# A decoder layer on one core: the last quarter of normed rows turned by transfers, and blocks, prepared sums and subtractions moved

## The chip, the core and the metric

The kernel runs on one core of one Trainium2 chip, as one program. The metric is the device time of one execution in microseconds, the median of several runs. The engines are named as in the profile: PE (TensorE, matmuls; PEld is its weight load), DVE (VectorE), ACT (ScalarE), POOL (GpSimd) and SP (SyncE, which here issues DMAs). A name such as L426 is a line of the kernel file.

## The reference

One layer of a decoder, all in float32, for 256 tokens (S) of width 2048 (D):

```
h = LN(alpha*h + 0.5*swiglu(h, w_ffn1_gu, w_ffn1_down))           # first feed-forward, FF = 5632
rq, rk, rv, rg, aq, ak, av, gate_r, gate_a = split(h @ w_in)
ro = head_norm(retention_chunkwise(rotary(rq), rotary(rk), rv))   # 8 heads, 128 / 256 wide
ret = (silu(rg) * ro) @ w_ret_out
att = sliding_window_attention_sinks(rotary(aq), rotary(ak), av) @ w_att_out
h = LN(alpha*h + (sigmoid(gate_r)*ret + sigmoid(gate_a)*att) @ w_mix_out)
h = LN(alpha*h + 0.5*swiglu(h, w_ffn2_gu, w_ffn2_down))
h = LN(alpha*h + sigmoid(h @ w_ple_gate) * (p @ w_ple_proj))
```

LN is a layer norm over the 2048 columns of a token, so a product that follows one needs the normed rows turned: tokens go from the partitions to the free axis.

## The kernel before, in words

**Products in three parts.** Each weight arrives by a DMA of 512 KB (128 partitions x 1024, "raw", `r...`), is cast on ACT to a rounded high part (`h...`, L130), and DVE subtracts to get the low part (`l...`, L134). A product is then three matmuls: high x high, high x low and low x high (L424 to L426), 512 columns each. A *pair* ("P") is two such chunks for one pair of k, 24 matmuls. A *transferred* unit ("T") has one of its two chunks get its low part in another way: ACT multiplies the raw weight by −1 (L139) and POOL issues a DMA that adds the raw weight (L140). A *seven* ("S") does the work of a pair with seven products in place of eight, 21 matmuls, from sums of weight quarters that DVE makes (`uf`, `vf`, `luf`, `lvf`, L214 to L223). A *prepared* unit ("D") is a seven whose sums were made earlier, in spare time, by `sums_ahead`, and put in DRAM.

**Stages.** First feed-forward: gate and up in eleven blocks of 512 columns (f1 j = 0 to 10, 5 to 459 us in the trace), down in two passes (to 689). Then the norm, the mixers (values `rv`, queries and keys `rqk`, gates `rg`, attention, `gt`, `ga`, `ma`, `mr`), the product with w_mix_out (`mo`, to 1446), a norm, the second feed-forward (f2, 1454 to 2136), a norm, and the embedding (`pg`, to the end). Each block of gate/up is given by a pattern of eight letters over the eight pairs of k (`gu_units`), for example PTSSPSST.

**Order.** Nothing is reordered at run time: each engine works through its instructions as written. A planner in the kernel's Python writes them. `plan` lists the units in the order in which PE uses them. After each unit that PE has been given, `fill` issues the next loads and the next casts and subtracts ("makes") as long as there is room (`slots_for_weights(slots, ahead, far)`: `ahead` is how many matmuls' worth of made weights may stand ready). Jobs put with `along(n, job)` and generators in `lazy` (tables, prepared sums) are given one step after each unit that PE has been given (`run_side`).

**A norm.** The class `Norm` combines the sums of a last block with the residual (`combine`), takes statistics, centres and scales the rows on DVE (`normal`, L660, L665), and turns them for the next product: PE transposes 128 x 128 pieces against an identity into PSUM (`lnps`, L677), ACT casts them to the high part (L105), DVE subtracts for the low part (L106). A norm has 16 such k for two halves of tokens, 32 transposes, in groups of four. These steps are put between the first matmuls of the next product by a list of events, (number of the step, what): a pair (t, c) is "turn quarter c of token half t", "more" centres and scales further rows, "go" lets `fill` run again. While a norm runs, that is held quiet. `held_out` runs the last block before a norm for one token half first, then for the other, so that the first half's norm can begin early.

**Turning by transfer.** Elsewhere (the blocks of the feed-forward, L947 to L967) rows are turned without PE: ACT copies the two 16-bit words of each value apart (`words_of`, L953), a transposing DMA on SP's queue turns them (`turn_words`, L959), and ACT joins the words (`join_words`, L967).

## Time and profile before

| | |
|---|---|
| median of 3 runs | 2243.78 us (2241.16 to 2244.8) |
| the profiled execution | 2240.34 us, span 2238.5 us, granted clock 0.999 |
| PE busy | 2226.3 us, 99% of the span, 10180 matmuls |
| DVE busy | 1992.1 us, 89%, 2646 instructions |
| ACT busy | 1414.8 us, 63%, 1672 instructions |
| POOL busy | 44.1 us, 2% |
| DMA | 558.71 MB, mean 250 GB/s; q1 (SP's loads) 71.0% and q0 (POOL's) 5.9% of 16 engines' span |

In rows of the timeline the columns are start, duration, engine, line, operation, out<-in, and in brackets how long the engine was idle ahead of it and what it waited for; several instructions of a kind in a row stand together (x8). In rows of waits they are the waiting engine, tile and line, who released it, and the time in total, the number of times and the longest. In rows of a tile they are durations in ns (least, median, largest), then first and last start. Names with a number (f19s, f210s) are feed-forward 1, block 9, and feed-forward 2, block 10; `s` is the PSUM bank of the sevens' products.

### The profile page before, as it was taken

The page shows a single profiled execution, that of the slowest core. Times are in us where ns is not written, and L with a number is a line of the kernel's source. Part 1 is how long each engine was busy: PE and PEld are TensorE (multiplying, and loading weights), DVE is VectorE, ACT ScalarE, POOL GpSimd, SP SyncE. Part 2 cuts the span into 40 slices and gives each one's busy share as a digit, 9 for nine tenths or more (in the row PEclk, how much of TensorE's full clock was granted, in tenths as well). Part 3 has the DMA queues.
Part 4 walks back from the last instruction along what each step waited for, and adds up shares of the span by engine and source line. Part 5 has one row for each costly group of instructions (what it writes and reads, how often), then busy time and mean ns, then how long its engine had stood idle before and what let it go on. Part 6 is the DMA issues. An engine that isn't in the chain of part 4 may idle for free.

```text
span 2238.5 us, 28874 instructions
## 1 busy us (share of the span) xinstructions
PE 2226.3 (99%) x10180; PEld 1842.2 (82%) x10180; DVE 1992.1 (89%) x2646; ACT 1414.8 (63%) x1672; POOL 44.1 (2%) x57
## 2 busy tenths in 40 slices
PE   9999999999999999999999999999999999999998
PEld 8888888888888888888788888788888888888887
DVE  7999999989999999898779778789998899899887
ACT  6776766786654644666866555456666677866543
POOL 0000000000000000000000000000000000000000
PEclk9999999999999999999999999999999999999999
DMA  9788887896776778986657569787979978867772
GB/s 315 227 261 244 226 259 234 229 262 235 253 273 260 252 266 308 305 257 205 189 165 248 172 215 326 263 291 253 314 250 273 311 233 248 262 224 252 284 268 72
DMA packets 288826, 558.71 MB, mean 250 GB/s; under 512 B 87964, under 2 KB 92444, under 8 KB 288680
## 3 DMA queue, kind: packets, MB, share of 16 engines
q1 hardware_dynamic: 279784, 529.11, 71.0%
q0 software_dynamic: 6912, 25.17, 5.9%
q10 hardware_dynamic: 1984, 2.58, 0.3%
q8 instruction: 80, 1.31, 0.2%
q14 instruction: 66, 0.54, 0.1%
HBM read 484.43 MB, written 29.36 MB: 230 GB/s over the span
## 4 chain that ended last, share of the span: by engine, by line
PE 88%; DVE 7%; DMA 3%; issue 2%; ACT 1%; ACTq 0%; DVEq 0%; POOL 0%; SPq 0%; POOLq 0%
PE rqk L375 3%; PE f1g L425 3%; PE f1g L424 3%; PE f1g L426 3%; PE f2g L425 2%; PE f2g L426 2%; PE f2g L424 2%; PE f1u L425 2%; PE f1u L424 2%; PE f1u L426 2%; PE f2u L425 2%; PE f2u L426 2%; PE f2u L424 2%; PE aqk L375 2%; PE gt L424 1%
## 5 line engine op out<-in xcount | busy, mean ns | idle before, releaser
L130 ACT CAST hf_gu<-rf_gu 128x1024 fp32r<-128x1024 f32 x264 | 271.3, 1046 | 44.4 <-DMA rf_gu<-in_f_gu 42.8
L134 DVE TENSOR_TENSOR lf_gu<-rf_gu,hf_gu 128x1024 fp32r<-128x1024 f32 x236 | 281.7, 1218 | 14.7 <-ACT hf_gu L130 13.4
L130 ACT CAST hf_down<-rf_down 128x1024 fp32r<-128x1024 f32 x145 | 148.4, 1047 | 61.4 <-DMA rf_down<-in_f_down 52.9
L134 DVE TENSOR_TENSOR lw_in_f<-rw_in_f,hw_in_f 128x1024 fp32r<-128x1024 f32 x140 | 167.1, 1218 | 3.5 <-ACT hw_in_f L130 3.3
L130 ACT CAST hw_in_f<-rw_in_f 128x1024 fp32r<-128x1024 f32 x140 | 141.9, 1050 | 24.9 <-DMA rw_in_f<-in_w_in_f 17.5
L134 DVE TENSOR_TENSOR lf_down<-rf_down,hf_down 128x1024 fp32r<-128x1024 f32 x125 | 149.6, 1218 | 7.6 <-ACT hf_down L130 6.9
L220 ACT CAST hvf_gu<-vf_gu 128x1024 fp32r<-128x1024 f32 x76 | 80.2, 1055 | 85.0 <-DVE vf_gu L219 77.2
L217 ACT CAST huf_gu<-uf_gu 128x1024 fp32r<-128x1024 f32 x76 | 80.0, 1053 | 54.5 <-DVE uf_gu L215 50.0
L222 DVE TENSOR_TENSOR luf_gu<-uf_gu,huf_gu 128x1024 fp32r<-128x1024 f32 x76 | 92.5, 1217 | 1.0 <-ACT huf_gu L217 1.0
L223 DVE TENSOR_TENSOR lvf_gu<-vf_gu,hvf_gu 128x1024 fp32r<-128x1024 f32 x76 | 92.5, 1217 | 0.0
L424 PE MATMUL f1g<-hf_gu,xt 128*128 128x512 f32 x232 | 90.7, 391 | 0.0
L426 PE MATMUL f1g<-lf_gu,xt 128*128 128x512 f32 x232 | 90.5, 390 | 0.0
L425 PE MATMUL f1g<-hf_gu,xt 128*128 128x512 f32 x232 | 90.5, 390 | 0.0
L424 PE MATMUL f2g<-hf_gu,ht 128*128 128x512 f32 x214 | 83.5, 390 | 0.0
L426 PE MATMUL f2g<-lf_gu,ht 128*128 128x512 f32 x214 | 83.3, 389 | 0.0
L425 PE MATMUL f2g<-hf_gu,ht 128*128 128x512 f32 x214 | 83.3, 389 | 0.0
L424 PE MATMUL f1u<-hf_gu,xt 128*128 128x512 f32 x192 | 74.7, 389 | 0.0
L425 PE MATMUL f1u<-hf_gu,xt 128*128 128x512 f32 x192 | 74.7, 389 | 0.0
L426 PE MATMUL f1u<-lf_gu,xt 128*128 128x512 f32 x192 | 74.7, 389 | 0.0
L424 PE MATMUL f2u<-hf_gu,ht 128*128 128x512 f32 x168 | 65.7, 391 | 0.0
L426 PE MATMUL f2u<-lf_gu,ht 128*128 128x512 f32 x168 | 65.4, 389 | 0.0
L425 PE MATMUL f2u<-hf_gu,ht 128*128 128x512 f32 x168 | 65.4, 389 | 0.0
(1624 smaller groups left out, 6799.7 us busy)
## 6 DMA issues: line engine op xcount, KB each, us to landing
rf_gu<-in_f_gu SPq DMA_DIRECT2D x360, 512.0 KB
rf_down<-in_f_down SPq DMA_DIRECT2D x176, 512.0 KB
rw_in_f<-in_w_in_f SPq DMA_DIRECT2D x148, 512.0 KB
rw_rv<-in_w_rv SPq DMA_DIRECT2D x32, 512.0 KB
rw_ret<-in_w_ret SPq DMA_DIRECT2D x32, 512.0 KB
rw_mix<-in_w_mix SPq DMA_DIRECT2D x32, 512.0 KB
rw_pg<-in_w_pg SPq DMA_DIRECT2D x32, 512.0 KB
lf_gu<-rf_gu POOLq DMA_DIRECT2D x28, 512.0 KB, 7.9
```

Source lines behind the costliest of these rows:

```text
L130: act.copy(self.hi, self.raw)
L134: dve.tensor_tensor(self.lo, self.raw, self.hi, ALU.subtract)
L217: act.copy(uh, u)
L220: act.copy(vh, v)
L222: dve.tensor_tensor(ul, u, uh, ALU.subtract)
L223: dve.tensor_tensor(vl, v, vh, ALU.subtract)
L375: pe.matmul(ps[f], hi[:, kk, f * P : (f + 1) * P], rhs(k), start=k == 0, stop=k == n_k - 1,)
L424: pe.matmul(o, al, bh, start=first, stop=False)
L425: pe.matmul(o, ah, bh, start=False, stop=False)
L426: pe.matmul(o, ah, bl, start=False, stop=self.left == 0)
```

## The change

What it does, part by part:

- **Last quarter by transfer.** In the three norms whose rows are turned, k = 12 to 15 is no longer turned by PE. An event "part" has ACT copy the words, SP transpose by DMA, ACT join into a raw tile and cast it, and DVE subtract. 24 of 96 transposes go.
- **Joined blocks.** Behind the first norm the value blocks 0 and 3 (`rv0`, `rv3`) run as pairs over k in place of one after the other; behind the last norm the embedding blocks 0 and 1 do so too, and the final sigmoid, products, loading of norm vectors and scaling of these two blocks come behind both. The value blocks 1 and 2 use PPSSPSSP in place of PSPSSPSP.
- **Moved prepared sums and table.** The ten items of `sums_ahead` and the rotary tables start elsewhere: the retention table at step 6 of the first down pass instead of 11; items 0 and 1 and the attention table in `rqk` instead of before and in the value blocks, 2 to 4 in `rg`, 5 and 6 in the gates `gt`, 7 in `ma`; 8 and 9 stay at `mo`. Room for weights is cut to 14 while sums run in `gt` and `ma`.
- **Mixing norm.** Ahead of it, 112 in place of 136 matmuls' worth of weights may stand ready; two makes that stood before the norm are events 11 and 12 within it, and `fill` is held quiet for the last four units of the first token half instead of two.
- **Late blocks.** Gate/up blocks from j = 9 (f1) and j = 6 (f2) on use PTSSTSST in place of PTSSPSST: one more transferred unit. Blocks 5 and 7 of f2 use PSDSSDSP in place of PPSDSDSP: one more seven, one pair fewer.

The diff, cut to its core:

```diff
...
+LATE = {"f1": 9, "f2": 6}
...
+                elif what == "part":
+                    self.part()
...
+        def part(self):
+
+            parts = words_of(self.y[3].rearrange("p t n -> p (t n)"), f"ln{self.i}")
+            along(0, lambda: self.go_over(parts))
+
+        def go_over(self, parts):
+            turns = turn_words(parts, f"ln{self.i}")
+            along(2, lambda: self.join(turns))
+
+        def join(self, turns):
+            raw = slot([P, 4, S], F32, f"lnraw{self.i}")
+            join_words(raw, turns)
+            act.copy(self.new[:, 12:, :S], raw)
+            along(0, lambda: dve.tensor_tensor(self.new[:, 12:, S:], raw, self.new[:, 12:, :S], ALU.subtract))
...
+            if j > 4:
+                return units_of("PSDSSDSP", SEVEN, AHEAD[j])
             return units_of(*(("PPSDSDSP", SEVEN[:3]) if j % 2 else ("PPSSDSSP", SEVEN)), AHEAD[j])
-        return units_of("PTSSPSST", SEVEN)
+        return units_of("PTSSTSST" if j >= LATE[name] else "PTSSPSST", SEVEN)
...
-                    (3, (1, 0)), (5, "more"), (5, (1, 1)), (7, (0, 2)), (8, (1, 2)), (9, (0, 3)), (10, (1, 3)), (10, "go"),
+                    (3, (1, 0)), (5, "more"), (5, (1, 1)), (7, (0, 2)), (8, (1, 2)), (9, "part"), (10, "go"),
...
-            if u == 11 and name == "f1":
+            if u == 6 and name == "f1":
...
-    VALUE_UNITS = units_of("PSPSSPSP", (0, 1, 2, 3))
+    VALUE_UNITS = units_of("PPSSPSSP", (0, 1, 2, 3))
...
+    outer_keys = lambda n, p: ("w_rv", 3 * n, p)
...
-        ps = banks("rv0")
-        sums = [[Sum(ps[t], KD)] for t in range(2)]
-        norm.first([(("w_rv", 0, c), 2 * c, 0) for c in range(FRONT)], rhs, sums, (
-            (5, (1, 0)), (6, (1, 1)), (8, (1, 2)), (8, "more"), (9, (1, 3)), (10, (0, 3)), (10, "go"),
+        ps = [banks("rv0"), banks("rv3")]
+        sums = [[Sum(ps[n][t], KD) for n in range(2)] for t in range(2)]
+        norm.first([(outer_keys(n, p), 2 * p, n) for p in range(FRONT_PAIRS) for n in range(2)], rhs, sums, (
+            (5, (1, 0)), (6, (1, 1)), (8, (1, 2)), (8, "more"), (9, "part"), (10, "go"),
         ))
         slots_for_weights(24)
-        for c in range(FRONT, KD // 2):
-            u = take(("w_rv", 0, c))
-            tokens_chunk(u.chunk, 2 * c, rhs, [sums[t][0] for t in range(2)], (0, 1))
-            done(u)
-        values(0, ps)
-        for g in range(2):
-            made[g] = forms_of([ht[:, 4 * g : 4 * g + 4, :]], f"rvf{g}")
+        for p in range(FRONT_PAIRS, KD // 2):
+            if p in (4, 6):
+                g = p // 2 - 2
+                made[g] = forms_of([ht[:, 4 * g : 4 * g + 4, :]], f"rvf{g}")
+            for n in range(2):
+                u = take(outer_keys(n, p))
+                tokens_chunk(u.chunk, 2 * p, rhs, [sums[t][n] for t in range(2)], (0, 1))
+                done(u)
+                run_side()
+        for n in range(2):
+            values(3 * n, ps[n])
         ahead = [(gu_keys("f2", j)(0, p), gu_keys("f2", j)(1, p)) for j in AHEAD for p in AHEAD[j]]
-        lazy.append(sums_ahead(ahead[:2], 3, 2))
-        lazy.append(rotary_table("a"))
-        lazy.append(sums_ahead(ahead[2:5], 2, 2))
-        lazy.append(sums_ahead(ahead[5:8], 2, 3))
-        ps = banks("rv3")
-        tokens_out(("w_rv", 3), KD, rhs, ps)
-        values(3, ps)
         slots_for_weights(22)
         for n, v in enumerate(mixer_block("rvs", VALUE_UNITS, value_keys, rhs)):
             values(1 + n, v)
         made.clear()
         slots_for_weights(14)
+        lazy.append(rotary_table("a"))
+        lazy.append(sums_ahead(ahead[0:2], 2, 2))
...
+        lazy.append(sums_ahead(ahead[2:5], 2, 3))
...
-        slots_for_weights(18)
+        slots_for_weights(14)
+        lazy.append(sums_ahead(ahead[5:7], 0, 2))
         sig = []
         for j in range(4):
+            if j == 3:
+                slots_for_weights(18)
...
-        slots_for_weights(20)
+        slots_for_weights(14)
+        lazy.append(sums_ahead(ahead[7:8], 0, 2))
...
-        slots_for_weights(26, 136, 160)
+        slots_for_weights(26, 112, 160)
...
-        norm.run(steps, lhs, ((8, (0, 0)), (10, (0, 1)), (10, "sums")), (2, 3))
+        norm.run(steps, lhs, ((8, (0, 0)), (10, (0, 1)), (10, "sums"), (11, "make"), (12, "make")), (2, 3), 4)
...
+        pair = [banks(f"pg{blk}") for blk in range(2)]
+        sums = [[Sum(pair[n][t], KD) for n in range(2)] for t in range(2)]
+        steps = [(("w_pg", n, p), 2 * p, n) for p in range(FRONT_PAIRS) for n in range(2)]
+        norm.first(steps, lhs, sums, (
+            (1, (0, 2)), (1, "sums"), (5, (1, 0)), (6, (1, 1)), (7, (1, 2)), (7, "more"), (8, "part"), (10, "go"),
+        ))
+        slots_for_weights(24)
+        for p in range(FRONT_PAIRS, KD // 2):
+            for n in range(2):
+                u = take(("w_pg", n, p))
+                tokens_chunk(u.chunk, 2 * p, lhs, [sums[t][n] for t in range(2)], (0, 1))
+                done(u)
+                run_side()
+        sgs = [slot([P, 2, 512], F32, f"sg{blk}") for blk in range(2)]
+        for at, (blk, t) in enumerate(((0, 0), (1, 0), (0, 1), (1, 1))):
+            along(at, lambda blk=blk, t=t: finish(blk, pair[blk][t], sgs[blk], t))
+        run_side()
+        g, b = ln_vectors(3)
+        two_rows = small.tile([P, 96], F32, tag="plnm", bufs=1, name="plnm")
+        pool.memset(two_rows, 0.0)
+        ident_r = small.tile([P, P], F32R, tag="identr", bufs=1, name="identr")
+        act.copy(ident_r, ident)
+        along(4, rows_of_vectors)
+        along(5, lambda: scale(0))
+        along(7, lambda: scale(1))
...
```

What this does to the order of instructions shows at three places. The first is DVE in the gate/up block f1 j = 9 (`lf_gu` is a low part, `uf`, `vf` the sums of a seven; the first number behind the name is the half, the second the pair of k). Before:

```order
432 L223 TENSOR_TENSOR lvf_gu_0_1_3449<-vf_gu_0_1_3445,hvf_gu_0_1_3448 128x1024
433 L134 TENSOR_TENSOR lf_gu_0_6_3479<-rf_gu_0_6_3410,hf_gu_0_6_3442 128x1024
434 L134 TENSOR_TENSOR lf_gu_1_6_3513<-rf_gu_1_6_3427,hf_gu_1_6_3477 128x1024
435 L214 TENSOR_TENSOR uf_gu_0_2_3542<-rf_gu_1_2_3463 128x512
436 L215 TENSOR_TENSOR uf_gu_0_2_3542<-rf_gu_0_2_3461,rf_gu_1_2_3463 128x512
```

And now:

```order
432 L225 TENSOR_TENSOR lvf_gu_0_1_3450<-vf_gu_0_1_3447,hvf_gu_0_1_3449 128x1024
433 L136 TENSOR_TENSOR lf_gu_0_6_3480<-rf_gu_0_6_3410,hf_gu_0_6_3442 128x1024
434 L216 TENSOR_TENSOR uf_gu_0_2_3543<-rf_gu_1_2_3466 128x512
435 L217 TENSOR_TENSOR uf_gu_0_2_3543<-rf_gu_0_2_3464,rf_gu_1_2_3466 128x512
436 L218 TENSOR_TENSOR vf_gu_0_2_3544<-rf_gu_0_2_3464,uf_gu_0_2_3543 128x512
```

One of the two subtracts between the sevens of pairs 1 and 2 is gone from DVE.

The second is DVE ahead of the mixing norm and within it (`lf_gu` are the first weights of f2; `mixy` the rows, L1584 and L1612 the combine). Before:

```order
1689 L134 TENSOR_TENSOR lf_gu_0_1_12925<-rf_gu_0_1_12921,hf_gu_0_1_12923 128x1024
1690 L134 TENSOR_TENSOR lf_gu_1_1_12943<-rf_gu_1_1_12939,hf_gu_1_1_12941 128x1024
1691 L134 TENSOR_TENSOR lf_gu_0_2_12961<-rf_gu_0_2_12957,hf_gu_0_2_12959 128x1024
1692 L134 TENSOR_TENSOR lf_gu_1_2_12979<-rf_gu_1_2_12975,hf_gu_1_2_12977 128x1024
1693 L1584 SCALAR_TENSOR_TENSOR mixy_12864<-mixy_12864,mo_12866 128x512
```

And now:

```order
1686 L136 TENSOR_TENSOR lf_gu_0_1_12955<-rf_gu_0_1_12915,hf_gu_0_1_12935 128x1024
1687 L136 TENSOR_TENSOR lf_gu_1_1_12973<-rf_gu_1_1_12917,hf_gu_1_1_12953 128x1024
1688 L1612 SCALAR_TENSOR_TENSOR mixy_12862<-mixy_12862,mo_12864 128x512
...
1713 L669 SCALAR_TENSOR_TENSOR mixy_12314<-mixy_12314,rstd_13098,ln_b_0_12699 128x256
1714 L136 TENSOR_TENSOR lf_gu_0_2_13113<-rf_gu_0_2_12919,hf_gu_0_2_12971 128x1024
1715 L136 TENSOR_TENSOR lf_gu_1_2_13125<-rf_gu_1_2_12939,hf_gu_1_2_13111 128x1024
```

The subtracts of pair 2 went from before the combine of the first token half to behind the first scaled columns of the second.

The third is ACT behind the first norm, in the changed kernel only, since the steps are new (`ln0w`, `lnraw` and the last cast are the new quarter; `rvf0h` is the cast of sums that DVE makes for the value blocks):

```order
513 L976 COPY ln0w<-f1y_5606 128x1024 x2
514 L132 CAST hw_rv_3_6255<-rw_rv_3_5974 128x1024
...
521 L132 CAST hw_rv_7_6283<-rw_rv_7_6180 128x1024
522 L659 ACT_TABLE_LOAD
523 L659 ACTIVATE few<-few 128x1
524 L506 CAST rvf0h<-sums 128x1024
525 L990 COPY lnraw_6363<-ln0t 128x1024 x2
526 L791 CAST ht_5967<-lnraw_6363 128x4x256
527 L132 CAST hw_rv_7_6379<-rw_rv_7_6200 128x1024
```

Eight casts of weights (rows 514 to 521), a table load and the cast that waits for DVE's sums now stand between the copies of the words and the joins.

More of the change, by code (lines that the diff above doesn't have):

```diff
@@ L440, in tokens_out @@
         for c in range(n_k // nk):
+            if before is not None:
+                before(c)
             u = take(key + (c,))
@@ L791, in first @@
                 self.follow(len(steps) + j + 1, events)
[L792 removed]
+            assert not events and len(set(self.turned)) == 6
             self.put_away()
@@ L1708, in embedding @@
             key = ("w_pg", blk)
[L1709 to L1722 removed]
+            if blk < 3:
                 for c in range(KD // 2):
@@ L1807, in layer @@
         plan_ffn("f2")
-        for blk in range(4):
+        block_units([("P", p) for p in range(KD // 2)], lambda n, p: ("w_pg", n, p))
+        for blk in range(2, 4):
             plan_tokens(("w_pg", blk), KD)
```

39 lines of the change are left out of this document (7 added, 32 removed).

## The prediction

> **What bounds the kernel now.** I read the page's totals first, then the list of what TensorE (PE) waited for, then the timeline around each of those waits.
>
> ```profile
> span 2238.5 us, 28874 instructions
> PE 2226.3 (99%) x10180; PEld 1842.2 (82%) x10180; DVE 1992.1 (89%) x2646; ACT 1414.8 (63%) x1672; POOL 44.1 (2%) x57
> PE 88%; DVE 7%; DMA 3%; issue 2%; ACT 1%; ACTq 0%; DVEq 0%; POOL 0%; SPq 0%; POOLq 0%
> ```
>
> PE is busy for 99% of the span and holds 88% of the chain, so an edit pays only if it removes PE instructions or a wait of PE. VectorE (DVE) at 89% is next: an edit that loads it can make a new wait. The waits of PE are short:
>
> ```profile
> PE lnps L677 <- DVE mixy L665: 1.9, 2, 1.4
> PE f19s L426 <- DVE luf_gu L222: 0.8, 1, 0.8
> PE f210s L426 <- DVE luf_gu L222: 0.5, 1, 0.5
> PE rvss L426 <- DVE lvw_rv L223: 0.2, 1, 0.2
> PE f210s L426 <- DVE lvf_gu L223: 0.2, 1, 0.2
> PE f19s L426 <- DVE lvf_gu L223: 0.2, 1, 0.2
> PE f28s L426 <- DVE lvf_gu L223: 0.2, 1, 0.2
> ```
>
> The change touches all seven: the mixing norm (1.9 us), the late gate/up blocks f1 j=9, f2 j=8 and j=10 (1.9 together), and the block of the values (0.2).
>
> **The change part by part.**
>
> *Transposes.* Eight of the 32 transposes of each of three norms leave PE.
>
> ```profile
> L677 PE MATMUL lnps<-ident,f1y x32: 270/273/327, 689.2 to 712.6; 128*128 128x128 f32 x32
> ...
> 712.32 0.60 PE L677 MATMUL lnps<-ident,f1y 128*128 128x128 f32 x4
> 712.67 0.48 PE L424 MATMUL rv<-hw_rv,ht 128*128 128x512 f32 x1
> 712.99 0.39 PE L425 MATMUL rv<-hw_rv,ht 128*128 128x512 f32 x1
> ```
>
> The last four transposes of this norm begin at 712.32, and the second matmul behind them at 712.99. Matmuls of this size start 0.23 us apart (rows of f2 below), so without the four it would have begun at 712.55: 0.44 us for a group, six groups, **−2.7 us** (0.27 us each by duration, 24 x 0.27 = 6.5, is the upper bound, but they overlap). What replaces them runs on other engines: two copies of 16-bit words (1.04 us each), a transposing DMA, two joins (1.35 each), a cast (1.05) and a subtract on DVE (1.22).
>
> ```profile
> L953 ACT COPY f18w<-evw x2: 1042/1042/1043, 393.9 to 394.9; 128x1024 uint16<-128x1024 uint16 x2
> L967 ACT COPY f1a<-f18t x2: 1340/1346/1353, 424.4 to 425.6; 128x1024 uint16<-128x1024 uint16 x2
> ...
> L959 SPq EVENT_SEMAPHORE  x38: 17/28/7854, 67.8 to 1920.8; - x38
> ...
> L959 SPq DMA_TRANSPOSE f24t<-f24w x1: 8740/8740/8740, 1685.3 to 1685.3; - x1
> L959 SPq DMA_TRANSPOSE f25t<-f25w x1: 3630/3630/3630, 1724.8 to 1724.8; - x1
> ```
>
> The issue takes 3.6 to 8.7 us on SP's queue in these two rows, with a wait of up to 7.9 us ahead of it, and the loads of weights queue behind it. The new quarter serves k = 12 to 15, the end of the first pass over the rows. How much time it has in the first norm:
>
> ```profile
> 696.81 0.39 PE L424 MATMUL rv<-hw_rv,ht 128*128 128x512 f32 x1
> ...
> 711.31 0.75 DVE L665 SCALAR_TENSOR_TENSOR f1y<-f1y,rstd,ln_b 128x512 f32<-128x512 f32 x1
> ...
> 713.44 7.70 ACT L130 CAST hw_rv<-rw_rv 128x1024 fp32r<-128x1024 f32 x8
> 721.15 1.28 ACT L655 ACT_TABLE_LOAD   x1
> ...
> 727.30 1.05 ACT L502 CAST rvf0h<-sums 128x1024 fp32r<-128x1024 f32 x1 [3.69 <-DVE sums L501]
> ```
>
> With two blocks in pairs PE does 6 x 2 x 12 = 144 matmuls (32.6 us) and three groups of transposes (1.4) before it asks for k = 12: 696.8 + 34 = 730.8. The rows are ready at 712.06. ACT then stands in this order: words to 714.1, eight casts (7.7) and the table with what it needs (1.5) to 723.3, the cast of DVE's sums for rvf0 (it begins 4 us behind the last low part today; with DVE behind ACT as now, say 726 to 727), two joins to 729.7, a cast to 730.7; DVE's subtract ends at 731.9. So PE waits about **+1.1 us**; bounds 0 and 4.8, where the DMA has the long wait and the long issue together (7.9 + 8.7 = 16.6 us, 3.7 more than it has between 714.1 and 727). It is nearer 1 because the waits have a median of 28 ns.
>
> The other two norms are built alike: their last transposes stand equally deep in the first pass, 15.8 us behind its start here (712.6 − 696.8), so the quarter is asked for 34 − 15.8 = 18 us behind them. Words, DMA, joins, cast and subtract are 2.0 + 3.6 to 8.7 + 2.6 + 1.05 + 1.2 = 10.5 to 15.6 us, and no sums for a value block stand in the way: early by 2.4 to 7.5 us. Cost 0, up to 5.5 with the long wait.
>
> *f2 j = 5 and 7: one more seven-product unit each.* It takes 21 matmuls instead of 24, so 6 fewer in all.
>
> ```profile
> 1671.76 0.39 PE L426 MATMUL f2u<-lf_gu,ht 128*128 128x512 f32 x1
> ...
> 1672.44 0.39 PE L426 MATMUL f25s<-lf_gu,ht 128*128 128x512 f32 x1
> ```
>
> Three matmuls take 0.68 us: 0.227 x 6 = **−1.4 us**. DVE pays: a unit is five operations of 128x512 and three of 128x1024, in place of two of 128x1024.
>
> ```profile
> 1685.46 0.69 DVE L214 TENSOR_TENSOR uf_gu<-rf_gu 128x512 f32<-128x512 f32 x1 [4.43 <-DMA rf_gu<-in_f_gu]
> 1686.07 0.68 DVE L215 TENSOR_TENSOR uf_gu<-rf_gu,rf_gu 128x512 f32<-128x512 f32 x1
> ...
> 1672.00:1712.00 40.00, 40.00 (x178) 33.14 (x177) 33.69 (x42) 24.25 (x27) 0.88 (x1) 1.00 0.99 315
> ```
>
> Back to back a small one starts 0.61 us after its predecessor and a large one 1.15 (the two rows of 1442.44 and 1443.59 under the mixing norm): 5 x 0.61 + 1.15 = 4.2 us more per block. In the window of j = 5 (length, then busy time of PE, PEld, DVE, ACT, POOL, clock, DMA share, GB/s) DVE is busy 33.7 of 40 us, so 37.9 would still fit, but if it also waits 4.4 us for a load as it does now, it needs 42.3: 2.3 us behind; in j = 7 I take the same. Bounds: 0 (the wait shrinks as DVE comes later) and 2 x 2.3 = 4.6; I take **+1.5 us**, nearer the lower end, since PE does not wait at all there today and so has some lead.
>
> *Late blocks.* In f1 j = 9, 10 and f2 j = 6, 8, 9, 10 one low part goes from DVE to ACT and an adding transfer of POOL.
>
> ```profile
> 374.00:414.00 40.00, 38.99 (x171) 31.62 (x171) 39.23 (x48) 30.34 (x35) 2.01 (x3) 1.00 0.80 232
> ...
> 408.84 0.50 PE L426 MATMUL f19s<-luf_gu,f1fh 128*128 128x512 f32 x1 [0.84 <-DVE luf_gu L222]
> ```
>
> DVE is busy 39.2 of these 40 us and 0.84 late at 408.8; it gets 1.13 us back ahead of that unit. The same 1.13 covers j = 10 of f2 (0.5 + 0.2) and j = 8 (0.2). In the next part 1.9 us of waits are 2.3 from start to start; at that rate these 1.9 give **−2.3 us**; bounds 0 and −2.7.
>
> The added transfers: ACT has 9.7 us free in that window, and a multiply takes 1.06.
>
> ```profile
> DMA to landing us min/median/max: 5.3/7.9/9.8
> q0 software_dynamic: 6912, 25.17, 5.9%
> ```
>
> They land 7.9 us after their issue (5.3 to 9.8) and nothing of PE waits for one today. The unit at its new place is begun as many units ahead as the one at the block's end, which is no wait of PE now. Cost 0; the upper bound is 1.9 us (9.8 − 7.9) each, 11.4 for six.
>
> The Trainium skill has a rule against this: its page "SBUF — State Buffer", section "SBUF: two separate sides", says that a DMA issued from the GpSimd queue has its descriptors written by GpSimd, which is locked out while DVE runs a two-port operation, so the transfer only seems blocked by DVE and is best issued elsewhere. The trace does not bear it out here: 28 transfers landed within 5.3 to 9.8 us while DVE was at 0.84 and 0.98 in the two windows of such blocks that stand above. By the rule the six would land late and the sum would lose up to the 11.4 us above.
>
> *Mixing norm.* Before:
>
> ```profile
> 1442.44 1.23 DVE L134 TENSOR_TENSOR lf_gu<-rf_gu,hf_gu 128x1024 fp32r<-128x1024 f32 x1 [1.06 <-ACT hf_gu L130]
> 1443.59 0.68 DVE L1584 SCALAR_TENSOR_TENSOR mixy<-mixy,mo 128x512 f32<-128x512 f32 x1
> ...
> 1445.26 0.39 PE L426 MATMUL mo<-lw_mix,mixt 128*128 128x512 f32 x1
> 1447.03 0.44 PE L677 MATMUL lnps<-ident,mixy 128*128 128x128 f32 x2 [1.37 <-DVE mixy L665]
> 1447.94 0.33 PE L677 MATMUL lnps<-ident,mixy 128*128 128x128 f32 x1 [0.48 <-DVE mixy L665]
> ```
>
> The 24 matmuls of the second half end with 1445.26, so the first half's sums were complete at 1440.05. The combine stands behind two subtracts whose weights came late (the second is shown) and starts at 1443.59; the transposes follow 3.44 us later. Moved behind the norm, those two let the combine start at about 1440.4 and the transposes be ready at 1443.9, before PE is free at 1445.5. The gap from 1445.49 to 1447.03 (1.54) and the second of about 0.7 go: **−2.3 us**. The two subtracts are next needed by the third pair of f2's first block, about 2.4 us after the moved place gives them; cost 0, bound +2.3.
>
> *Values, prepared sums and table.*
>
> ```profile
> 742.00:784.00 42.00, 41.83 (x184) 34.03 (x183) 41.84 (x50) 25.67 (x29) 0.00 (x0) 1.00 0.76 259
> 1104.00:1147.00 43.00, 43.00 (x208) 33.34 (x207) 30.89 (x51) 33.71 (x57) 0.00 (x0) 1.00 0.68 199
> ```
>
> DVE is full in the values block (742 to 784), from which two prepared sums and a table leave: its wait of 0.2 us goes, **−0.2**. It is a quarter idle in the gates (from 1104), where two sums come in: 8 small operations and 4 large ones, 9.5 us of 12.1 idle, beside a DMA that has a third free. Cost 0, up to +1 if their loads delay those of the gates. The embedding blocks in pairs keep their matmuls: 0.
>
> Sum: −2.7 − 1.4 − 2.3 − 2.3 − 0.2 + 1.1 + 1.5 = **−6.3 us**. The profiled execution took 2240.34 us, 1.8 outside its span and 3.4 below the median of the runs; I expect 2234.0 in a profile like it and 2243.8 − 6.3 = **2237.5** as median.
>
> **The rivals.**
>
> *The join becomes the wait.* The transposing DMA has the long wait and the long issue in the first norm (3.7 us more) and in one of the others (7.9 − 2.4 = 5.5): 9.2 given back, 2246.7, within 0.2% of the median and a little above. For it: SP's queue is full of loads at a norm. Against: the median wait, and 13 us between words and join in the first norm.
>
> *Waits only move.* DVE's work is the same, so the 4.6 us of the late blocks and the mixing norm come back elsewhere; only PE's own 4.1 us count, less 1.1 at the first join: −3, 2241. For it: DVE at 89%. Against: DVE's idle time is where the work goes.
>
> *Slower: f2 j = 5 to 8 run out of loads.* The DMA share is 0.99 in j = 5 already, and j = 6 and 8 each add a transfer (5.9% of the span for 48 transfers is 2.75 us of all queues each). If each of the four blocks then waits as long as DVE waits for a load today (4.4), PE loses 17.6 in place of the 1.5: 2237.5 + 16 = 2253. It decides from 2 us a block on, where 8 − 1.5 takes the whole forecast, and from 3.1 a block the kernel is slower by 0.2%. Against: PE shows no wait in these blocks now.
>
> *The added transfers land late* (the mechanism under late blocks): 2237.5 + 11.4 = 2249.
>
> **How the numbers follow.** Forecast 0.62, join 0.10, waits move 0.15, out of loads 0.09, late transfers 0.04. About 0.2% (4.5 us) is what a measurement of this kernel tells from no change, so faster means under 2239.3. Faster: 0.56 of the forecast's 0.62 and 0.04 of "waits move", 0.60. Same: 0.06 + 0.11 + 0.08 of the join + 0.03 of the last two, 0.28. Slower: 0.02 of the join, 0.07 and 0.03, 0.12. The likeliest case has its own range: 2234.5 (the gains without a loss, −9.3 with the upper bound of the late blocks) to 2241 (the second blocks at 4.6, and the join half a microsecond more). To leave out 2 in 10 at most, the range reaches up to 2246, over the first two rivals, and down to 2232, two thirds of the way to the transposes' upper bound of 6.5.
>
> **What would show it.** PE's list has no more mixy wait over 0.5 us and no f19s, f210s wait; 24 transposes fewer; a new wait of PE for the DVE subtract of the raw quarter, near 730, of 0 to 2 us; f25s and f27s show waits under 2.2 us each. It is wrong if lf_gu transfers or rf_gu loads become what PE waits for in f2 j = 5 to 10, or if the second and third norms wait for their quarter.

## The result and the profile after

The changed kernel takes 2230.94 us (median of 4 runs, 2229.55 to 2232.14) beside 2242.74 us for the kernel before (4 runs, 2241.16 to 2244.8): a ratio of 0.9945, 95% interval 0.9933 to 0.9958. That is 11.8 us, where 6.3 were forecast; the time lies 1.1 us below the range. Timed once more in another session it was 2231.15 beside 2244.03 us (0.9942, 0.9926 to 0.9957). The two profiled executions stand only 8.2 us apart (2240.34 and 2232.14).

From the page of the changed kernel: the span, the busy time of the engines and the chain by engine.

```profile
span 2230.3 us, 28863 instructions
PE 2221.0 (100%) x10150; PEld 1838.2 (82%) x10150; DVE 1993.9 (89%) x2649; ACT 1434.9 (64%) x1691; POOL 49.2 (2%) x63
PE 92%; DVE 4%; ACT 2%; issue 1%; DMA 1%; SPq 0%; ACTq 0%; DVEq 0%
```

PE issues 30 matmuls fewer (24 transposes, 6 products); DVE fell from 7% of the chain to 4%. The list of what PE waited for, same kernel:

```profile
PE warm L1826 <- POOL ident masks.py:199: 1.4, 1, 1.4
PE rv L426 <- DVE ht L792: 0.8, 1, 0.8
PE f1g L428 <- DVE lf_gu L136: 0.3, 1, 0.3
...
PE f26s L428 <- DVE lvf_gu L225: 0.2, 1, 0.2
PE f26s L428 <- DVE luf_gu L224: 0.2, 1, 0.2
```

The waits of the mixing norm (mixy), of f19s, f210s, f28s and rvss are gone. The one new wait above 0.3 us is the forecast one for the new quarter (`ht` L792); f26s now waits twice 0.2 us. The timeline of ACT and of PE around it:

```profile
709.80 1.99 ACT L976 COPY ln0w<-f1y 128x1024 uint16<-128x1024 uint16 x2 [2.26 <-DVE f1y L669]
711.70 7.69 ACT L132 CAST hw_rv<-rw_rv 128x1024 fp32r<-128x1024 f32 x8
719.40 1.28 ACT L659 ACT_TABLE_LOAD   x1
...
723.62 1.05 ACT L506 CAST rvf0h<-sums 128x1024 fp32r<-128x1024 f32 x1 [2.73 <-DVE sums L505]
724.58 2.57 ACT L990 COPY lnraw<-ln0t 128x1024 uint16<-128x1024 uint16 x2
727.18 1.05 ACT L791 CAST ht<-lnraw 128x1024 fp32r<-128x1024 f32 x1
...
729.54 0.50 PE L426 MATMUL rv<-hw_rv,ht 128*128 128x512 f32 x1 [0.83 <-DVE ht L792]
```

This is the chain of the prediction step by step: words, eight casts, table, a wait for DVE's sums, joins, cast, and PE 0.83 us idle. The mixing norm, DVE and then PE:

```profile
1436.93 0.69 DVE L1612 SCALAR_TENSOR_TENSOR mixy<-mixy,mo 128x512 f32<-128x512 f32 x1 [2.49 <-PE mo L428]
...
1441.94 0.39 PE L428 MATMUL mo<-lw_mix,mixt 128*128 128x512 f32 x1
1442.17 0.60 PE L681 MATMUL lnps<-ident,mixy 128*128 128x128 f32 x4
```

The combine now waits for PE's own sums and for no weight, and the transposes follow the last matmul after 0.23 us. Windows of f2 j = 5 and 7 and of the late part of f1:

```profile
1665.00:1705.00 40.00, 40.00 (x178) 32.91 (x177) 37.55 (x46) 27.78 (x30) 1.72 (x2) 1.00 1.01 319
1746.00:1786.00 40.00, 39.86 (x176) 32.53 (x175) 39.45 (x48) 28.55 (x32) 1.61 (x2) 1.00 1.00 309
372.50:412.50 40.00, 40.00 (x179) 33.10 (x178) 37.53 (x46) 29.75 (x34) 2.27 (x3) 1.00 0.88 253
```

DVE is at 37.6 of 40 us in j = 5, as worked out (37.9); yet PE has no gap there. In j = 7 DVE is at 39.5, and PE misses 0.14 us. In f1 j = 9 DVE has 2.5 us free where it had 0.8.

### The profile page after: what moved, and what is told of

The parts are those of the page before. It is cut to its first block, busy times and chain, and to the rows that moved or that the text cites. A ratio compares the mean times of both kernels' runs of the same rounds, so it can differ in the third digit from the quotient of the medians.

```text
span 2230.3 us, 28863 instructions
## 1 busy us (share of the span) xinstructions
PE 2221.0 (100%) x10150; PEld 1838.2 (82%) x10150; DVE 1993.9 (89%) x2649; ACT 1434.9 (64%) x1691; POOL 49.2 (2%) x63
## 4 chain that ended last, share of the span: by engine, by line
PE 92%; DVE 4%; ACT 2%; issue 1%; DMA 1%; SPq 0%; ACTq 0%; DVEq 0%
PE f1g L428 3%; PE f1g L426 3%; PE f1g L427 3%; PE rqk L377 3%; PE f2g L426 2%; PE f2g L427 2%; PE f2g L428 2%; PE f1u L428 2%; PE f1u L426 2%; PE f1u L427 2%; PE f2u L427 2%; PE f2u L426 2%; PE f2u L428 2%; PE aqk L377 2%; PE gt L426 1%; PE f2d L428 1%
## 5 line engine op out<-in xcount | busy, mean ns | idle before, releaser
L136 DVE TENSOR_TENSOR lf_gu<-rf_gu,hf_gu 128x1024 fp32r<-128x1024 f32 x228 | 272.7, 1219 | 11.6 <-ACT hf_gu L132 10.8
L426 PE MATMUL f2g<-hf_gu,ht 128*128 128x512 f32 x208 | 81.1, 390 | 0.0
L427 PE MATMUL f2g<-hf_gu,ht 128*128 128x512 f32 x208 | 80.9, 389 | 0.0
L142 POOL DMA_DIRECT2D lf_gu<-rf_gu x34 | 29.5, 867 | 1707.4 <-DMA rf_gu<-in_f_gu 1097.0
L377 PE MATMUL rqk<-ht,hw_in_f 128*128 128x512 f32 x256 | 64.3, 392 | 0.0
L426 PE MATMUL f2u<-hf_gu,ht 128*128 128x512 f32 x160 | 62.5, 391 | 0.0
```

The costliest lines, as they stand in the source:

```text
L136: dve.tensor_tensor(self.lo, self.raw, self.hi, ALU.subtract)
L142: pool.dma_start(self.lo, self.raw.bitcast(F32R), accum_op=ALU.add)
L377: pe.matmul(ps[f], hi[:, kk, f * P : (f + 1) * P], rhs(k), start=k == 0, stop=k == n_k - 1,)
L426: pe.matmul(o, al, bh, start=first, stop=False)
L427: pe.matmul(o, ah, bh, start=False, stop=False)
```

## The experiments

Theory A: each part is worth what it takes off PE's stream and PE's list. Since the gain was larger, there were rivals: that the profiled execution of the kernel before was a short one of executions that vary, and where they vary.

### What each part is worth: one part at a time put back

**The changed kernel again.**

> The changed kernel itself, timed again beside the kernel before. Theory A (the gain is what left PE's stream and PE's list of waits): 8.2 us, the difference of the two profiles, so a ratio near 0.9963. Theory B (the profiled execution of the kernel before was a quick one, and its usual execution has waits that this profile does not show): 11 to 12 us, a ratio near 0.9948.

2231.15 us (5 runs, 2230.8 to 2232.07) beside 2244.03 (9 runs, 2240.66 to 2250.69). The ratio is B's. The changed kernel's runs lie within 1.3 us, those of before within 10.

Each part put back is compared with this 2231.15. From the spread of the runs I estimate 95% intervals of about 1 us either way for such a difference, 2.2 for the mixing norm and 2.6 for f2 j = 5 and 7, whose runs spread more. The last three parts were timed in another session than the changed kernel.

**Late blocks put back.**

```diff
-LATE = {"f1": 9, "f2": 6}
+LATE = {"f1": 11, "f2": 11}
```

> The changed kernel with PTSSPSST in all late gate/up blocks, as before. Theory A: about 2.4 us above the changed kernel, with the waits of f19s (about 1.0), f28s (0.2) and f210s (0.7) back in PE's list. Theory B: 4 us or more, because these blocks are where usual executions wait longer than that profile. Rival (the waits only move): within 0.5 us, with new waits elsewhere gone.

2232.44 us (5 runs), 1.3 above the changed kernel in the same session. f19s waits again, 0.8 us in the list and 1.0 from start to start; f28s and f210s do not. PE's list of this kernel:

```profile
PE f19s L428 <- DVE luf_gu L224: 0.6, 1, 0.6
...
PE f19s L428 <- DVE lvf_gu L225: 0.2, 1, 0.2
```

So the late pattern is worth its f1 half. The 2.3 us of the sum were 1 too many, and neither A's 2.4 nor the rival's 0.5 came. For f210s the reason is in the kernel before: its wait (0.5 + 0.2) stands in the first profile alone. The four others, below, have none there, and in them PE goes from f210s to the down product in 30.1 us in place of 31.2.

**Mixing norm put back.**

```diff
-        slots_for_weights(26, 112, 160)
+        slots_for_weights(26, 136, 160)
-        norm.run(steps, lhs, (..., (10, "sums"), (11, "make"), (12, "make")), (2, 3), 4)
+        norm.run(steps, lhs, (..., (10, "sums")), (2, 3))
```

> The changed kernel with the room of 136 ahead of the mixing norm, the two makes ahead of it and quiet for two units, as before. Theory A: 2.3 us above the changed kernel, with PE's mixy wait of 1.9 us back. Theory B: more than 3.5 us. Rival (the wait is gone for another reason, the moved prepared sums): within 0.5 us and no mixy wait.

2234.4 us (5 runs, 2233.0 to 2237.41): 3.3 above the changed kernel, and more widely spread. The wait is back, in PE's list and as the two gaps of the timeline, and the matmuls behind the gaps start 0.43 us apart in place of 0.23:

```profile
PE lnps L681 <- DVE mixy L669: 2.1, 2, 1.6
...
1443.98 0.44 PE L681 MATMUL lnps<-ident,mixy 128*128 128x128 f32 x2 [1.57 <-DVE mixy L669]
1444.90 0.69 PE L681 MATMUL lnps<-ident,mixy 128*128 128x128 f32 x2 [0.48 <-DVE mixy L669]
...
1446.24 0.63 PE L428 MATMUL pp<-lw_pp,pt 128*128 128x512 f32 x1
1446.67 0.63 PE L426 MATMUL pp<-hw_pp,pt 128*128 128x512 f32 x1
...
1448.54 0.40 PE L428 MATMUL pp<-lw_pp,pt 128*128 128x512 f32 x1
```

The mechanism is A's, the size between A's 2.3 and B's 3.5. There is a second cost in it, which neither theory had. The granted clock was 0.51 from 1445.0 to 1448.3 us. From the second pair of transposes (1444.90) to the next four (1449.47) PE took 4.57 us; in the first profile of the kernel before, at a clock of 1.00, it took 3.06 (1447.94 to 1451.00). So the lower clock cost 1.5 us on top of the gaps.

Two other profiles have such a stretch at this place: the fifth of the kernel before (0.54 from 1449.0 to 1452.5 us) and the one with the new f2 pattern alone (0.60 from 1448.0 to 1452.0). In these three the first gap was 1.57, 1.95 and 2.39 us. In the four other profiles of the kernel before it was 1.24 to 1.49, and the clock stayed at 1.00. Length alone does not decide: in the run with f2 j = 5 and 7 put back PE stood still for 3.26 us and the clock stayed at 1.00. What does decide stays open.

**Prepared sums, tables, value pattern put back** (r table at step 11, items 0 to 7 ahead of and in the value blocks, PSPSSPSP, rooms of 18 and 20).

```diff
-            if u == 6 and name == "f1":
+            if u == 11 and name == "f1":
...
+        lazy.append(sums_ahead(ahead[:2], 3, 2))
+        lazy.append(rotary_table("a"))
+        lazy.append(sums_ahead(ahead[2:5], 2, 2))
+        lazy.append(sums_ahead(ahead[5:8], 2, 3))
         slots_for_weights(22)
```

> The changed kernel with the prepared sums, the two tables, the value pattern and the room for weights where they were before (sums in the value blocks). Theory A (a part is worth what it takes off PE's list): 0.3 to 1 us above the changed kernel, with rvss (0.2) and f1y (0.4) back in PE's list. Theory B, in a new form (timings of the kernel before spread over 10 us and those of the changed kernel over 1.3, so one part removed a wait that most executions had and the two profiles of before do not show): if it is this part, 3 us or more above, with a spread of over 4 us.

2232.98 us (5 runs, 2231.71 to 2234.16), 1.8 above the changed kernel's 2231.15 of the session before. Two waits in its list:

```profile
PE lnps L681 <- DVE f1y L669: 0.4, 1, 0.4
...
PE ro L1318 <- DVE rsp L108: 0.2, 1, 0.2
```

The one at f1y must go with the table, the only one of these edits that stands ahead of the first norm: at step 11 its DVE work is closer to it. The prediction had seen only rvss (0.2), which did not come back. Beside the second profile of the changed kernel, f1y costs PE 0.7 us from start to start and `ro` 0.3; where the rest of the 1.8 lies is not shown. Not this part makes the spread of before.

**f2 j = 5 and 7 put back.**

```diff
-                return units_of("PSDSSDSP", SEVEN, AHEAD[j])
+                return units_of("PPSDSDSP", SEVEN[:3], AHEAD[j])
```

> The changed kernel with PPSDSDSP in f2 j = 5 and 7, as before: six matmuls more. Theory A: 1.4 us for the matmuls less about 0.9 of waits at f26s and f27s that go, so 0.3 to 0.8 us above the changed kernel. Rival (the extra sevens cost more than they save): 0.5 us or more below it. Theory B: 3 us or more above, widely spread.

2233.44 us (10 runs), 2.3 above the changed kernel, but from 2231.51 to 2240.64: four of ten above 2235. For the median A failed. In the blocks themselves it did not: from the first matmul of f24s to the first of f28s PE took 161.4 to 162.9 us in the six profiles with the old pattern (this one and the five of the kernel before; median 161.65) and 160.8 to 161.6 in nine with the new one (median 160.95), 0.7 us less. The profiled execution was one of the long ones (span 2237.3), and from f28s to the down product it took 117.7 us, the changed kernel 112.0 and 112.1. Its timelines show what happened there. POOL, SP, ACT and PE:

```profile
1842.67 0.86 POOL L142 DMA_DIRECT2D lf_gu<-rf_gu  x1 [11.66 <-DVE uf_gu L216]
...
1842.75 4.85 SPq L982 DMA_TRANSPOSE f28t<-f28w  x1
1847.78 12.38 SPq L121 DMA_DIRECT2D rf_gu<-in_f_gu  x8
...
1860.67 1.06 ACT L141 ACTIVATE lf_gu<-rf_gu 128x1024 fp32r<-128x1024 f32 x1 [11.14 <-DMA rf_gu<-in_f_gu]
1861.64 1.03 ACT L132 CAST hf_gu<-rf_gu 128x1024 fp32r<-128x1024 f32 x1
1862.57 0.58 ACT L537 COPY eve<-f29s 128x512 f32<-128x512 f32 x1
...
1863.20 0.50 PE L426 MATMUL f2g<-hf_gu,ht 128*128 128x512 f32 x1 [3.26 <-ACT eve L537]
```

An adding transfer of POOL and the transposing DMA of the block were issued within 0.1 us of each other. What the DMA engines moved in that stretch of 16 us, in 40 slices (busy tenths, then GB/s):

```profile
DMA  9204938999999998799999899997999897920498
GB/s 364 103 0 118 138 97 282 399 347 236 209 63 55 54 86 64 58 67 67 195 124 143 127 154 196 58 20 40 291 48 22 18 30 20 64 10 9 98 375 328
```

From 1846.4 to 1856 they are 70% busy or more and move mostly 20 to 150 GB/s. The loads of weights queue behind, ACT stands 11.14 us in front of one of them with the copy of a PSUM result (L537) behind it in its order, and PE waits 3.26 us for that. The forecast's rival of loads that run out had this consequence in it, but not this cause.

**All transposes back on PE** (events (0, 3) and (1, 3) in place of "part" in the three norms).

```diff
-(8, (1, 2)), (9, "part"), (10, "go"),
+(8, (1, 2)), (9, (0, 3)), (10, (1, 3)), (10, "go"),
```

> The changed kernel with all 96 transposes on PE as before, the joined blocks kept. Theory A: 2.7 us of transposes less 1.0 of the wait at the first join, so 1.7 us above the changed kernel. The upper bound by durations (24 x 0.27 us): 5.5 above. Theory B: 3 us or more above, widely spread.

2232.92 us (5 runs, 2232.12 to 2233.9), 1.8 above the changed kernel: A's 1.7. The wait for `ht` L792 is gone from its list. Beside the kernel of the next part, timed in the same session, which has neither the 24 transposes nor that wait, it is 3.1 above (2.7 by the sum).

### The wait for the new quarter

```diff
-            if p in (4, 6):
-                g = p // 2 - 2
+            if p in (6, 7):
+                g = p - 6
```

> The changed kernel with the sums of rvf0 and rvf1 issued at pairs 6 and 7 in place of 4 and 6, so that ACT's joins of the first norm no longer stand behind the cast that waits for DVE's sums. Theory A: the wait of PE for the new quarter (0.8 us in the list, 1.0 from start to start) goes and the kernel is 0.8 to 1.0 us faster than the changed one. Rival (the transposing DMA is what is late): no gain.

> The changed kernel with the sums of rvf0 and rvf1 at pairs 6 and 7, a second time, as the base of the next one. 2229 to 2231 us.

2229.82 us (5 runs, 2229.59 to 2230.45) and 2229.97 (5 runs, 2229.44 to 2230.44), 1.2 below the changed kernel's medians of other sessions; against the kernel before 0.9947 and 0.9945 (0.9933 to 0.9957). ACT around the join:

```profile
720.09 1.28 ACT L659 ACT_TABLE_LOAD   x1
721.38 0.21 ACT L659 ACTIVATE few<-few 128x1 f32<-128x1 f32 x1
721.93 2.57 ACT L990 COPY lnraw<-ln0t 128x1024 uint16<-128x1024 uint16 x2 [0.34 <-DMA ln0t<-ln0w]
```

The joins start at 721.93 in place of 724.58, wait 0.34 us for the DMA, and PE's wait is gone. So the sums in front were the cause; the transposing DMA had landed 0.34 us after ACT was free. This kernel beats both.

### Does a transposing DMA suffer from an adding transfer?

**The transposing DMA one unit later**, so that it comes nearer to POOL's issue.

```diff
-            later(3, lambda: turn(j, parts))
+            later(4, lambda: turn(j, parts))
```

> The changed kernel with each transposing DMA of the gate/up blocks issued one unit later (two loads of weights now stand ahead of it on SP's queue), so that it starts nearer to the adding transfer of POOL that follows it by 1.0 to 4.9 us today. Theory C (a transposing DMA and an adding transfer that start together hold each other up: in the profile of the kernel with PPSDSDSP in f2 j = 5 and 7 POOL's issue came 0.1 us before the transposing one, its packets ended 14.5 us after the issue in place of 4.6, and PE lost 3.4 us): at least one transposing DMA of the profile ends 10 us or more after its issue, and the times are 3 to 10 us longer or spread over 4 us and more. Rival (such a long transfer falls by chance and has nothing to do with POOL): within 1 us of the changed kernel, no long transfer.

2250.21 us (12 runs, 2236.7 to 2266.19), ratio to before 1.0041 (1.0021 to 1.0062): 19 us above the changed kernel, and spread over 30. In the profile PE waits for the transfers themselves. At the two waits shown below it lost 9.3 and 13.3 us beside the changed kernel, more than the 7.0 and 10.7 of the waits: the granted clock was 0.57 from 256 to 264 us and 0.54 from 1826 to 1841, so that matmuls behind the waits ran slower too. f2 j = 8, POOL, SP, PE and the list:

```profile
1812.78 0.89 POOL L142 DMA_DIRECT2D lf_gu<-rf_gu  x1 [15.12 <-DVE lf_gu L136]
...
1812.80 5.69 SPq L982 DMA_TRANSPOSE f27t<-f27w  x1
...
1835.37 0.80 PE L428 MATMUL f2u<-lf_gu,ht 128*128 128x512 f32 x1 [10.69 <-DMA lf_gu<-rf_gu]
...
PE f1u L428 <- DMA lf_gu<-rf_gu: 7.0, 1, 7.0
...
DMA to landing us min/median/max: 5.0/8.1/22.5
```

**The same with the second unit a pair.**

```diff
-        return units_of("PTSSTSST" if j >= LATE[name] else "PTSSPSST", SEVEN)
+        return units_of("PPSSTSST", SEVEN)
```

> The kernel with the transposing DMA of the gate/up blocks one unit later, as in the run before, but with the pattern PPSSTSST in all blocks that had a transferred unit as their second: the adding transfer that followed the transposing DMA now comes some 20 us after it (and the late blocks have one transferred unit fewer than the changed kernel). Theory C (both together hold each other up): no transposing DMA ends later than 10.5 us, the 7 to 11 us waits for lf_gu are gone, times of 2231 to 2236 with a spread under 4 us. Rival (a later transposing DMA does the harm by itself): 2245 and more, widely spread.

2243.91 us (11 runs, 2233.39 to 2251.59). My edit missed its aim: POOL's issues stand as near to the transposing DMAs as before (0.0 us at f18t), because the transfer that meets one is not the second unit's. So this run does not separate the two, and C's numbers for it failed.

**No transferred unit in the blocks at all.**

```diff
-        return units_of("PTSSTSST" if j >= LATE[name] else "PTSSPSST", SEVEN)
+        return units_of("PPSSPSSP", SEVEN)
```

> The changed kernel with the transposing DMA one unit later and no transferred unit in any gate/up block (PPSSPSSP), so no adding transfer is in flight beside a transposing DMA there; DVE has 2 to 3 low parts more in each block. Theory C: the packets of every transposing DMA of the gate/up blocks span less than 5.5 us, against 6 to 13 where they met a transfer in the two runs before, and PE waits for DVE (up to 2 us a block, 20 to 40 us in all), not for lf_gu transfers. Rival (a later transposing DMA is slow by itself): spans of 9 us and more again.

2251.02 us (4 runs, 2248.24 to 2254.6). It is slow, but with PE waiting for DVE: its list is a row of waits of 0.5 to 1.2 us for luf_gu in ten blocks, and has no wait for lf_gu transfers.

```profile
PE f26s L428 <- DVE luf_gu L224: 1.2, 1, 1.2
...
PE f16s L428 <- DVE luf_gu L224: 0.6, 1, 0.6
PE f19s L428 <- DVE luf_gu L224: 0.6, 1, 0.6
```

What tells the theories apart is how long the transposing DMAs take. Counted from the packet records of the traces: POOL's issue against the transposing one, the number of the transfer's packets that started while the transposing one's packets ran, and the time from the start of the first to the end of the last of the latter, in us:

```
kernel                    DMA    POOL issue  packets between  first to last
changed kernel            f28t   +1.6 us      15               2.3 us
before, fifth profile     f28t   +2.3         15               2.5
f2 j=5, 7 put back        f28t   -0.1        144              11.9
one unit later            f27t    0.0        268              19.9 (two transfers)
one unit later            f14t   +1.4        104              15.6
one unit later            f28t   -0.8        118               5.1
one unit later            f16t   -0.4         83               3.8
second unit a pair        f18t    0.0        144              15.8
second unit a pair        f29t   -0.5         79               3.1
no transferred unit       f27t   none          0               2.6
no transferred unit       f14t   none          0               5.2 (the longest of the blocks before f210t)
no transferred unit       f210t  +0.6 (down) 116               7.6
```

Without a transfer beside it no transposing DMA took more than 5.2 us at the same later place; in all profiles, each that took 6 or more had 40 and more packets of a transfer between its own. The longest took 19.9 us, not 13 as the last expectation has it. Meeting is needed in these profiles, not sufficient: some met 80 to 120 packets and took 3 to 5 us. Theory C is borne out as far as that; what decides between 3 and 20 us stays open.

**The transposing DMA one unit earlier**, together with the late sums.

```diff
-            later(3, lambda: turn(j, parts))
+            later(2, lambda: turn(j, parts))
```

> The same with every transposing DMA of the gate/up blocks one unit earlier than in the changed kernel, farther ahead of the adding transfer. Theory C: no collision is left, but few there are in the changed kernel either, so within 1 us of the one above and no wider. Rival (an earlier transposing DMA only waits for its words on SP's queue and holds the loads behind it): 1 to 4 us slower, with waits for loads in f1.

2229.87 us (5 runs, 2228.71 to 2230.03) beside 2229.97 in the same session: no difference that these runs can tell. The two profiles of the changed kernel show no meeting of 40 packets or more that an earlier place could remove.

### Why the executions of before vary

> The kernel before, profiled once more. Theory A: a span within 1 us of 2238.5 and the same list of waits. Theory B: a span of 2240 to 2243, with PE waits that the first profile lacks.

> The kernel before, profiled a third time, to see one of its longer executions (timed ones lie between 2238.7 and 2250.7 us). Theory C: where the execution is over 2242 us, a transposing DMA ends 10 us or more after its issue, with packets of an adding transfer between its own, and PE waits behind it. Rival: a long execution has its extra time in the mixing norm (mixy over 4 us) or in f1 j = 9 and f2 j = 10.

> The kernel before, profiled a fourth time; as for the third.

Single profiled executions of 2238.73, 2239.6 and 2240.31 us: all short, the mixing norm's wait at 2.0, 1.8 and 1.7 us, f26s between 0.2 and 1.0. No long one was caught, and the difference of the profiles stood.

> The kernel before, unchanged, timed as if it were a new one beside the timings of before that every comparison uses. Theory D (its executions vary): the same median as those timings, 2242 to 2244 us, spread over 5 us, ratio 1.000. Theory E (the timings of before that stand beside every other kernel are some 3 us longer than those of the same kernel run in the place of a new one, as its four single profiled executions of 2238.7 to 2240.3 us suggest): a median of 2239 to 2240.5 us, ratio near 0.9985.

2242.57 us (11 runs, 2241.29 to 2244.78) beside 2241.92: ratio 1.0004 (0.9995 to 1.0012). Theory E falls; the executions of before do vary, and this time the profile caught one of 2243.37 us. Its list of PE's waits, and DVE and ACT at the mixing norm:

```profile
PE lnps L677 <- DVE mixy L665: 2.4, 2, 1.9
...
PE f1g L424 <- ACT hf_gu L105: 1.2, 1, 1.2
...
PE lnps L677 <- DVE f2y L665: 0.4, 1, 0.4
...
1442.62 1.05 ACT L130 CAST hf_gu<-rf_gu 128x1024 fp32r<-128x1024 f32 x1 [1.35 <-DMA rf_gu<-in_f_gu]
...
1443.70 1.23 DVE L134 TENSOR_TENSOR lf_gu<-rf_gu,hf_gu 128x1024 fp32r<-128x1024 f32 x1 [1.18 <-ACT hf_gu L130]
1444.85 0.68 DVE L1584 SCALAR_TENSOR_TENSOR mixy<-mixy,mo 128x512 f32<-128x512 f32 x1
```

3.0 us more than the first profile's span: 1.1 at the start (a wait for the first weights' cast), 2.1 between `mo` and f2, 0.9 at the last norm, and 1.6 less in f1 j = 9 and f2 j = 10; the rest is small. Of the 2.1, 0.6 are a longer first gap (2.1 from start to start in place of 1.5) and 1.5 the granted clock of 0.54 behind it. No transposing DMA was long in it. So of the rival named with the third profile the place holds, the mixing norm, but neither its 4 us of mixy wait (2.4 here) nor f1 j = 9 and f2 j = 10. The wait hangs on when a load lands: the cast in front of DVE's subtract waits 1.35 us for one here.

The timed executions fit that. Of the 87 of the kernel before that were timed beside the experiments, the 22 with a mean granted clock of 0.998 or less have a median of 2243.7 us, the 65 others one of 2241.9. That is part of the spread, not all of it, and where the clock fell is known for the profiled ones alone.

**The f2 j = 5 and 7 pattern alone in the kernel before.**

```diff
+            if j > 4:
+                return units_of("PSDSSDSP", SEVEN, AHEAD[j])
             return units_of(*(("PPSDSDSP", SEVEN[:3]) if j % 2 else ("PPSSDSSP", SEVEN)), AHEAD[j])
```

> The kernel before with PSDSSDSP in f2 j = 5 and 7 alone. Theory A (a part is worth what it takes off PE): 6 matmuls, 1.4 us, less up to 1 us of waits at f26s and f27s, so 0.4 to 1.4 us faster than before in the median. Theory D (with the old pattern the place of f2's transposing DMAs against the adding transfers varies from execution to execution, and with the new one it does not): 3 to 5 us faster in the median, with a spread under 4 us.

2240.09 us (11 runs, 2237.08 to 2241.14) beside 2242.81 (21 runs, 2238.88 to 2248.1): 0.9983 (0.9974 to 0.9992), 2.7 us. It stands between A's 1.4 and D's 3, with a spread of 4 in place of 9 us. Both from before and from the changed kernel this part is worth 2.3 to 2.7 us, of which 1.4 are the six matmuls, less some 0.7 of waits. In the profile of this kernel the mixy wait is 2.6 us, with the lower clock behind it, so what the pattern ended was not that. Where the other 2 us were in the kernel before no profile shows.

## Why the prediction was right in direction and too small

Its terms against what putting the part back cost (medians against 2231.15 us; for the intervals see above):

| part | forecast | measured |
|---|---|---|
| transposes and the new wait | −2.7 + 1.1 = −1.6 | −1.8 |
| f2 j = 5, 7 | −1.4 + 1.5 = +0.1 | −2.3 (−2.7 alone) |
| late blocks | −2.3 | −1.3 |
| mixing norm | −2.3 | −3.3 |
| values, sums, tables | −0.2 | −1.8 |
| sum | −6.3 | −10.5 of 11.8 to 12.9 timed |

- *Transposes.* Right in both halves: PE's loss per group and the chain behind the first norm, whose cause the late sums confirmed. The other two norms had no wait, as said. Without the new wait the transposes came to 3.1, forecast 2.7. The rival of the late join did not come.
- *f2 j = 5 and 7: the step that failed most.* The sum set +1.5 us of new waits against the 1.4 of the six matmuls; put back, the part is worth 2.3. Two things were wrong. The waits came to about half: in the blocks themselves PE gained 0.7 of the 1.4. The DVE load came out as worked out, but "if it also waits 4.4 us for a load as it does now" did not hold: the longest waits of DVE in j = 5 are 1.68 and 0.63 us, both for ACT and neither for a load. What remained were waits at f26s (0.2 and 0.2), as large as in the kernel before, whose f26s waited 0.2 to 1.0 us in three of its other profiles. And the old pattern had a cost that the one profile did not show, the wider spread. With the rest of the change around it that cost was a meeting of two DMAs, some 5.7 us in the execution that was profiled; in the kernel before its place stays open.
- *Late blocks.* The mechanism was right in f1, where the wait went. In f2 the term counted about 1 us at f210s that the first profile had and the four others did not.
- *Mixing norm.* Right place, right order, 1.0 too small. The term held the two gaps and not the lower clock that followed them where the first was 1.57 us or longer: 1.5 us in the profile of the put-back. The first profile, with a gap of 1.37, could not show it.
- *Values, sums and tables.* Mis-sized by 1.6: the forecast looked at the block that the sums leave and not at the norm ahead of it, where the table's DVE work held f1y up (0.4 in the list of before, which I had read and tied to no edit), nor at `ro`. These two are 1.0 of the 1.8; the rest is not shown.
- *Added transfers.* Cost 0 as said; they land after 6.0 to 10.3 us (median 7.9). By the rule of the Trainium skill's page "SBUF — State Buffer", section "SBUF: two separate sides", it is DVE's two-port operations that hold their descriptors back. No run here shows whether DVE ran such operations in these blocks, so the landing times speak neither for the rule nor against it, and the prediction read too much into them. The long ones here (14 to 22 us in the experiments) were those that met a transposing DMA.
- *The base.* The forecast was made against one profile, 2240.34 us, and took its waits as those of the median. Five profiles of that kernel lie between 2238.7 and 2243.4, its timed runs between 2237.2 and 2250.7. The forecast for a profile (−6.3) missed by 1.9, that for the median by 5.5. The difference is time that the usual execution of before has and its first profile lacks. Shown of it is the mixing norm, by its wait and the lower clock behind it, and, in a changed kernel, the meeting of two DMAs; for the rest of the spread of before (its runs above 2244) no profile was caught, and it stays open. The joined blocks were not tried apart, since without them PE asks for the turned quarter 72 matmuls (16.3 us) sooner.

## What to carry to other kernels

A wait on a load's landing that stands in one profile is one draw, and so is the clock behind it: where an engine's next instruction in order waits for a DMA, ask what that costs when the load is later, and compare the spread of the timed runs with the one profile. An operation that needs no late weight should not stand behind one that does (moving two subtracts, with less room ahead and a longer quiet, is worth 3.3 us). And before two kinds of DMA are issued near each other, try them an instant apart: here one unit of place was worth 19 us.

## What was not expected of the hardware

A transposing DMA (256-byte packets) and an adding transfer of 512 KB that are in flight together can take the transposing one up to 19.9 us and let through mostly 20 to 150 GB/s while the DMA engines read as 70 to 100% busy; apart they need 2.2 to 5.2 and about 4 us of packets. The spread of the timed runs (2231.5 to 2240.6 us with f2 j = 5 and 7 put back) suggests that it happens in some executions of one program and not in others; one execution each was profiled.

After a gap of PE of 1.57 to 2.39 us at the mixing norm the granted clock was near 0.5 for some 3.4 us and cost 1.1 to 1.6 us more than the gap itself. After gaps of 1.24 to 1.49 us it stayed at 1.00.
